# Low parts of the weights by a negation on ACT and an adding DMA, in place of a subtraction on DVE or POOL

## The chip, the cores and the metric

The kernel runs on one core of a Trainium2 chip. The metric is the device time of one execution in microseconds. Three runs of the kernel before gave 1173.53, 1174.44 and 1174.82 us; their median is 1174.44 us.

## What is computed

The reference is a two-layer trunk on 512 tokens of width 1024. Layer 0 is a gated short convolution beside a 4-head attention to 256 memory rows; then an MLP with a squared ReLU. After it, shared keys and values are made from the residual stream. Layer 1 (called layer B here) is differential attention over these keys beside memory attention, and again the MLP:

```python
for l in range(DEPTH):
    h = rmsnorm(x, norm_mix[l])
    proj = h @ (a_w_in[l] if l < N_A_LAYERS else b_w_q[j])
    ...
    main = short_conv_mixer(...) or diff_attention(q1, q2, k1, k2, v, lam)
    mo = memory_attention(qm, mem_n, w_mem_kv[l], ...)
    x = x + concatenate([main, mo]) @ w_o[l]
    x = x + square(relu(rmsnorm(x, norm_mlp[l]) @ w_up[l])) @ w_down[l]
    if l == N_A_LAYERS - 1:
        kv = rmsnorm(x, kv_norm) @ w_kv
```

Everything is float32, and the kernel keeps float32 accuracy by splitting each operand of a product into a high part (rounded to the type fp32r) and a low part (what the rounding left).

## The kernel before

All weights lie in DRAM in the order of their use, cut into **units**: eight 128x128 blocks that make one 128-row output tile. `UNITS` lists them: queries, convolution, memory keys and values, output projection, `up` and `dn` of the first MLP, then `qB`, `qk`, `kk`, `kv` for layer B, `wo1`, `wo2`, and the second MLP. A unit has two **halves** of four blocks (128x512 elements, 256 KB).

`dma_to` loads a unit into a tile `raw` (three buffers), one load of 512 KB from the queue of SP (L231) or two of 256 KB (L235). For the kinds `qB`, `kv`, `qk`, `kk`, POOL multiplies each loaded half in place by a gain (L241).

`prep_to` makes a half ready for TensorE: ACT copies `raw` into `wh`, rounded (L258), and then `wl = raw - wh` is one subtraction (L260). It runs on DVE, but on POOL for `wo1` and for the first `up` unit of the second MLP (`side`). `wh` and `wl` have four buffers each. Each half is prepared three halves ahead of its use (`AHEAD`), so the buffers that a preparation writes are those of the half that has just been used up. A unit's load is asked for one unit ahead of the preparation, and it waits until the last reader of the `raw` tile three units back is done.

`product` issues three matmuls for each block, into one PSUM bank: high by high (L276), the activations' low part by `wh` (L277), and the activations' high part by `wl` (L278). A half takes twelve matmuls of 512 columns.

Attention, norms and roots are generators with due times (`later`, `drive`), which put their instructions between the blocks of products. In layer B, POOL also does the rotary part of queries and keys (L926 to L928, behind a shuffle on DVE, L925) and clears tiles for the attention (L662, L663); in `wo1` it adds the residual (L955, L956). Each engine's queue takes its instructions in one order, which the framework sets when the kernel is built.

Of the kernel before, what the change touches and what calls it, by code (L numbers as in the profile page):

```python
# [10 lines left out]
F32 = mybir.dt.float32  # L11
F32R = mybir.dt.float32r
AF = mybir.ActivationFunctionType
ALU = mybir.AluOpType
# [20 lines left out]
WO_B = (2, 3)  # L35
SEG = 4
AHEAD = 3
LO_ON_POOL = ("wo1",)
WARM = 9

SUMS, ROOTS, NEXT_ROOT, VT = 5, 8, 3, 2
# [20 lines left out]
def _unit_list():  # L62

    u = []
    u += [("qmA", t, KT) for t in range(2)]
    for m in range(NH):
        if m == MEMA:
            u += [("mkv", 0, t, KT) for t in range(4)]
        if m == MEMB:
            u += [("mkv", 1, t, KT) for t in range(4)]  # L70
        u += [("win", CONV + m * P, KT), ("win", 2 * CONV + m * P, KT), ("win", m * P, KT)]
    u += [("woA", d, KT) for d in range(KT)]

    def mlp(l):
        r = []
        for q in range(NF):
            r += [("up", l, q * KT + f, KT) for f in range(KT)]
            r += [("dn", l, q, d, KT) for d in range(KT)]
        return r

    u += mlp(0)
    u += [("qB", 768 + t * P, KT) for t in range(2)]
    for p, t in LAYER_B:
        if t < 4:
            u += [("qk" if t < 2 else "kk", p * P + (t % 2) * 64, KT)]
        else:
            u += [("kv", 768 + (2 * p + t - 4) * P, KT)]
    u += [("wo1", i, KT) for i in range(len(WO1) // KT)]
    u += [("wo2", i, KT) for i in range(len(WO2) // KT)]
    u += mlp(1)  # L90
    return u


UNITS = _unit_list()
# [95 lines left out]
def trunk_kernel(ctx: ExitStack, tc: tile.TileContext, xT, memT, wall, cst, shp, csn, out):  # L190
    nc = tc.nc
    act, dve, pool, pe = nc.scalar, nc.vector, nc.gpsimd, nc.tensor
# [23 lines left out]
    side = next(i for i, u in enumerate(UNITS) if u[:2] == ("up", 1))  # L216
# [5 lines left out]
    def dma_to(n, between=()):  # L222
        between = list(between)
        while st["dma"] <= min(n, len(UNITS) - 1):
            i = st["dma"]
            kind, nb = UNITS[i][0], UNITS[i][-1]
            r = wpool.tile([P, KT, P], F32, tag="raw", name="raw", bufs=3)
            src = wall[OFFS[i] : OFFS[i] + P * P * nb].rearrange("(p b n) -> p b n", p=P, n=P)
            step = SEG if i < 2 or kind in ("qB", "kv", "qk", "kk") else nb
            if step == nb:  # L230
                nc.sync.dma_start(out=r[:, :nb, :], in_=src)  # L231
            for b0 in range(0, nb, step):
                rs = r[:, b0 : min(nb, b0 + step), :]
                if step < nb:
                    nc.sync.dma_start(out=rs, in_=src[:, b0 : min(nb, b0 + step), :])  # L235
                    for f in between[:2]:
                        f()
                    between = between[2:]
                if kind in ("qB", "kv", "qk", "kk"):
                    g0 = C_MIX1 if kind in ("qB", "qk") else C_KV  # L240
                    pool.tensor_tensor(  # L241
                        out=rs, in0=rs,
                        in1=cs[:, g0 + b0 : g0 + b0 + step].unsqueeze(2).to_broadcast([P, step, P]),
                        op=ALU.mult)
            st["raw"][i] = r
            st["dma"] += 1

    def prep_to(n):
        while st["prep"] <= min(n, len(halves) - 1):
            i, h = halves[st["prep"]]  # L250
            dma_to(i + 1)
            r = st["raw"][i]
            b0, b1 = h * SEG, min(UNITS[i][-1], h * SEG + SEG)
            rs = r[:, b0:b1, :]
            wh = wpool.tile([P, SEG, P], F32R, tag="wh", name="wh", bufs=4)
            wl = wpool.tile([P, SEG, P], F32R, tag="wl", name="wl", bufs=4)
            n_ = b1 - b0
            act.activation(out=wh[:, :n_, :], in_=rs, func=AF.Copy)  # L258
            eng = pool if i == side or UNITS[i][0] in LO_ON_POOL else dve
            eng.tensor_tensor(out=wl[:, :n_, :], in0=rs, in1=wh[:, :n_, :].bitcast(F32), op=ALU.subtract)  # L260
            st["w"][(i, h)] = (wh, wl)
            st["prep"] += 1

# [2 lines left out]
    def weights(b):  # L266

        i, b = cur["u"] + b // KT, b % KT
        prep_to(first[(i, b // SEG)] + AHEAD)
        wh, wl = st["w"][(i, b // SEG)]  # L270
        return wh[:, b % SEG, :], wl[:, b % SEG, :]
# [8 lines left out]
    def gemm_pieces(ps, srcs, order=range(KT), step=1, cols=slice(None)):  # L280

        u = cur["u"]
        cur["u"] += cols.stop in (None, S)
        for j, b in enumerate(order):
            prep_to(first[(u, b // SEG)] + AHEAD)
            wh, wl = (w_[:, b % SEG, :] for w_ in st["w"][(u, b // SEG)])
            product(ps, (wh, wl), [x_[:, cols] for x_ in srcs[b]], j == 0, j == len(order) - 1)
            if j % step == step - 1:
                yield
# [742 lines left out]
```

## Time and profile before

| | before |
|---|---|
| median of three runs | 1174.44 us |
| the profiled execution, its own time | 1173.49 us |
| its span, first to last instruction | 1171.7 us |
| busy: PE / DVE / ACT / POOL | 1140.6 / 697.4 / 526.3 / 191.2 us |
| the 16 DMA engines, share of the span in the queue of SP | 27.7% |
| subtractions on DVE and on POOL (L260) | 370 and 14 |

Busy times are sums of the instructions of an engine. PE is TensorE; its matmuls are pipelined, so that a row of some 390 ns stands for one that begins every 0.22 us or so. The word "released by" means that a semaphore of that instruction ended the wait. Times within the execution count from the start of the span.

### The profile page before, as it was taken

What the parts mean: (1) busy time and instruction counts of PE and PEld (TensorE: products, weight loads), DVE (VectorE), ACT (ScalarE), POOL (GpSimd) and SP (SyncE); (2) the same over time, 40 slices, a digit from 0 to 9 for tenths busy, and PEclk for the clock granted to TensorE, in tenths of its full rate; (3) what the DMA queues carried; (4) which work ended last, traced back from release to release, by engine and by line L of the source; (5) the groups of instructions that cost most, each with busy time, mean ns of one, the idle gap of its engine ahead of it and who ended that gap; (6) DMA issues with size and microseconds to landing.
All of it is one profiled execution on the core that took longest, in us unless ns stands there. A gap on an engine that the chain in (4) does not pass through costs nothing.

```text
span 1171.7 us, 14335 instructions
## 1 busy us (share of the span) xinstructions
PE 1140.6 (97%) x5343; PEld 931.3 (79%) x5343; DVE 697.4 (60%) x1124; ACT 526.3 (45%) x1013; POOL 191.2 (16%) x171
## 2 busy tenths in 40 slices
PE   8999999999999999999999889999999999999998
PEld 6888988888888888888777566767788888888887
DVE  7878664543443443446789999877743443443442
ACT  6655444432332432444556566676532432432431
POOL 3100002000000000005573744375200000000000
PEclk9999999999999999999999999999999999999999
DMA  8331323223223223232211111112232232322332
GB/s 270 107 121 60 118 99 100 98 90 105 93 92 106 90 97 101 90 107 91 91 54 37 55 55 42 50 55 72 90 108 91 95 103 91 106 92 92 106 109 72
DMA packets 35287, 108.38 MB, mean 93 GB/s; under 512 B 3985, under 2 KB 5521, under 8 KB 35217
## 3 DMA queue, kind: packets, MB, share of 16 engines
q1 hardware_dynamic: 35216, 107.47, 27.7%
q8 instruction: 42, 0.69, 0.2%
q14 instruction: 29, 0.23, 0.1%
HBM read 105.35 MB, written 2.10 MB: 92 GB/s over the span
## 4 chain that ended last, share of the span: by engine, by line
PE 82%; DVE 12%; ACT 2%; issue 1%; POOL 1%; DMA 0%; SPq 0%; DVEq 0%; POOLq 0%; ACTq 0%
PE g L276 26%; PE g L277 26%; PE g L278 26%; DVE wl L260 2%; DVE sl L490 1%; DVE pm L705 1%; DVE ql L344 1%; DVE dnb L697 1%; PE sc L576 1%; ACT pm L700 1%; DVE dsm L703 1%; DVE ra L413 1%; DVE xl L429 1%; PE msc L576 1%; DVE mp L619 1%
## 5 line engine op out<-in xcount | busy, mean ns | idle before, releaser
L258 ACT ACTIVATE wh<-raw 128x512 fp32r<-128x512 f32 x384 | 241.8, 630 | 484.0 <-PE g L277 427.2
L260 DVE TENSOR_TENSOR wl<-raw,wh 128x512 fp32r<-128x512 f32 x370 | 268.5, 727 | 175.6 <-ACT wh L258 175.2
L276 PE MATMUL g<-xh,wh 128*128 128x512 f32 x816 | 324.0, 397 | 0.4 <-DVE x L992 0.4
L277 PE MATMUL g<-xl,wh 128*128 128x512 f32 x816 | 321.0, 394 | 1.9 <-DVE xl L429 1.8
L278 PE MATMUL g<-xh,wl 128*128 128x512 f32 x816 | 319.6, 392 | 0.0
L276 PE MATMUL g<-hh,wh 128*128 128x512 f32 (+1 forms) x632 | 246.0, 389 | 1.8 <-ACT hh L343 1.8
L277 PE MATMUL g<-hl,wh 128*128 128x512 f32 (+1 forms) x632 | 244.9, 387 | 0.0
L278 PE MATMUL g<-hh,wl 128*128 128x512 f32 (+1 forms) x632 | 244.7, 387 | 0.0
L276 PEld LDWEIGHTS g<-xh,wh 128*128 128x128 f32 x816 | 154.3, 189 | 35.9 <-issue 2.7
L277 PEld LDWEIGHTS g<-xl,wh 128*128 128x128 f32 x816 | 154.3, 189 | 35.5 <-DVE xl L429 4.9
L278 PEld LDWEIGHTS g<-xh,wl 128*128 128x128 f32 x816 | 154.3, 189 | 32.3
L276 PEld LDWEIGHTS g<-hh,wh 128*128 128x128 f32 x632 | 119.1, 188 | 27.2 <-ACT hh L343 2.1
L278 PEld LDWEIGHTS g<-hh,wl 128*128 128x128 f32 x632 | 119.0, 188 | 24.0
L277 PEld LDWEIGHTS g<-hl,wh 128*128 128x128 f32 x632 | 119.1, 188 | 23.8 <-DVE hl L344 0.4
L762 DVE TENSOR_TENSOR x<-x,g 128x512 f32<-128x512 f32 (+1 forms) x65 | 44.2, 680 | 104.8 <-PE g L278 104.8
L752 DVE SCALAR_TENSOR_TENSOR v<-g,rstd 128x512 f32<-128x512 f32 x64 | 44.2, 691 | 90.6 <-PE g L278 90.6
L448 POOL TENSOR_TENSOR acc<-acc,sqf 128x512 f32<-128x512 f32 x18 | 25.2, 1398 | 368.3 <-ACT sqf L436 368.0
L755 DVE TENSOR_TENSOR hl<-a,hh 128x512 fp32r<-128x512 f32 x64 | 44.3, 693 | 37.8 <-ACT a L754 37.8
L241 POOL TENSOR_TENSOR raw<-raw,cs 128x512 f32<-128x512 f32 x40 | 46.7, 1186 | 34.1 <-DMA raw<-in_wall_dram 32.0
L753 ACT ACTIVATE hh<-v 128x512 fp32r<-128x512 f32 x64 | 40.4, 632 | 19.3 <-DVE v L752 19.3
L754 ACT ACTIVATE a<-v 128x512 f32<-128x512 f32 x64 | 39.4, 615 | 0.0
L700 ACT ACTIVATE pm<-sc,dnb 128x128 f32<-128x128 f32 (+3 forms) x48 | 25.0, 523 | 23.7 <-DVE dnb L697 23.6
(279 smaller groups left out, 1112.1 us busy)
## 6 DMA issues: line engine op xcount, KB each, us to landing
raw<-in_wall_dram SPq DMA_DIRECT2D x170, 512.0 KB, 3.5
raw<-in_wall_dram SPq DMA_DIRECT2D x44, 256.0 KB, 2.9
x<-in_xT_dram SPq DMA_DIRECT2D x8, 256.0 KB, 5.3
out_dram<-x SPq DMA_DIRECT2D x7, 256.0 KB, 2.0
mraw<-in_memT_dram SPq DMA_DIRECT2D x4, 256.0 KB, 5.8
rope<-in_csn_dram SPq DMA_DIRECT2D x2, 512.0 KB, 5.3
ind<-in_shp_dram SPq DMA_DIRECT2D x1, 256.0 KB, 5.6
out_dram<-x SPq DMA_DIRECT2D x2, 128.0 KB, 1.7
```

What stands on the lines that cost most here:

```text
L241: pool.tensor_tensor(out=rs, in0=rs, in1=cs[:, g0 + b0 : g0 + b0 + step].unsqueeze(2).to_broadcast([P, step, P]), op=ALU.mult)
L258: act.activation(out=wh[:, :n_, :], in_=rs, func=AF.Copy)
L260: eng.tensor_tensor(out=wl[:, :n_, :], in0=rs, in1=wh[:, :n_, :].bitcast(F32), op=ALU.subtract)
L276: pe.matmul(out=ps, lhsT=wh, rhs=xh, start=start, stop=False)
L277: pe.matmul(out=ps, lhsT=wh, rhs=xl, start=False, stop=False)
L278: pe.matmul(out=ps, lhsT=wl, rhs=xh, start=False, stop=stop)
L700: act.activation(out=pm[:, m, 0:n], in_=sc[m][:, 0:n], func=AF.Exp, bias=nb[:, m : m + 1], accum_out=sm[:, m : m + 1])
L752: dve.scalar_tensor_tensor(out=v, in0=ps, scalar=0.0, in1=rstd, op0=ALU.max, op1=ALU.mult)
L753: act.activation(out=hh, in_=v, func=AF.Square)
L754: act.activation(out=a, in_=v, func=AF.Square)
L755: dve.tensor_tensor(out=hl, in0=a, in1=hh.bitcast(F32), op=ALU.subtract)
L762: dve.tensor_tensor(out=x[d][:, c], in0=x[d][:, c], in1=ps[:, c], op=ALU.add)
```

## The change

For every half, ACT first writes `-raw`, rounded to fp32r, into `wl`; then a DMA issued from the queue of POOL adds `raw` to `wl` in place, which leaves the same rest; then ACT makes `wh` as before. No subtraction is left on DVE or POOL, and `LO_ON_POOL` goes.

```diff
-LO_ON_POOL = ("wo1",)
...
             n_ = b1 - b0
+            act.activation(out=wl[:, :n_, :], in_=rs, func=AF.Copy, scale=-1.0)
+            pool.dma_start(out=wl[:, :n_, :].bitcast(F32), in_=rs, accum_op=ALU.add)
             act.activation(out=wh[:, :n_, :], in_=rs, func=AF.Copy)
-            eng = pool if i == side or UNITS[i][0] in LO_ON_POOL else dve
-            eng.tensor_tensor(out=wl[:, :n_, :], in0=rs, in1=wh[:, :n_, :].bitcast(F32), op=ALU.subtract)
```

The line numbers move by one or two: in the changed kernel the negation is L259, the adding DMA L260, the rounding copy L261, the gain on POOL L240. The queues change as follows. In the rows, numbers tell one tile from another, and a name in brackets is a semaphore: `DMAHW` of a DMA of SP, `DMASW` of an adding DMA, the others of an engine.

POOL at the start of the program, before (the squares of the first five tiles of `x`, then the gate of a convolution):

```order
L663 MEMSET tl_5555 128x128
L438 ISA
L438 TENSOR_TENSOR acc_193<-x_105 128x512 [waits DMAHW2_49]
L438 TENSOR_TENSOR sqf_195<-x_106 128x512 [waits DMAHW3_49]
L438 TENSOR_TENSOR sqf_198<-x_107 128x512 [waits DMAHW5_49]
L438 TENSOR_TENSOR sqf_201<-x_108 128x512 [waits DMAHW6_49]
L438 TENSOR_TENSOR sqf_204<-x_109 128x512 [waits DMAHW0_49]
L829 TENSOR_TENSOR qp_441<-qp_441,qp_393 128x512 [waits DVE_49]
```

POOL at the same place, now:

```order
L664 MEMSET tl_5779 128x128
L260 DMA wl_251<-raw_132 128x512 [waits DMAHW1_49,Activation_49]
L439 ISA
L439 TENSOR_TENSOR acc_193<-x_105 128x512 [waits DMAHW2_49]
L439 TENSOR_TENSOR sqf_195<-x_106 128x512 [waits DMAHW3_49]
L439 TENSOR_TENSOR sqf_198<-x_107 128x512 [waits DMAHW5_49]
L439 TENSOR_TENSOR sqf_201<-x_108 128x512 [waits DMAHW6_49]
L439 TENSOR_TENSOR sqf_204<-x_109 128x512 [waits DMAHW0_49]
L260 DMA wl_256<-raw_132 128x512 [waits DMAHW4_49,Activation_49]
L260 DMA wl_261<-raw_139 128x512 [waits DMAHW7_49,Activation_49]
L260 DMA wl_266<-raw_139 128x512 [waits DMAHW2_49,Activation_49]
```

The first adding DMA stands ahead of the squares, the next three behind all five of them.

POOL where the gains of the first units of layer B are multiplied in (units `qB` and `qk`), before:

```order
L241 TENSOR_TENSOR raw_4709<-raw_4709,cs_95 128x512 [waits DMAHW6_49,DVE_49]
L241 TENSOR_TENSOR raw_4709<-raw_4709,cs_95 128x512 [waits DMAHW7_49]
L241 TENSOR_TENSOR raw_4765<-raw_4765,cs_95 128x512 [waits DMAHW0_49,DVE_49]
L241 TENSOR_TENSOR raw_4765<-raw_4765,cs_95 128x512 [waits DMAHW1_49]
L241 TENSOR_TENSOR raw_4814<-raw_4814,cs_95 128x512 [waits DMAHW2_49,DVE_49,Pool_49]
L241 TENSOR_TENSOR raw_4814<-raw_4814,cs_95 128x512 [waits DMAHW3_49]
```

POOL at the same place, now (the units' tiles are, in order, raw_4762, raw_4808, raw_4854, raw_4913, raw_4971):

```order
L260 DMA wl_4838<-raw_4762 128x512 [waits Activation_49]
L240 TENSOR_TENSOR raw_4854<-raw_4854,cs_95 128x512 [waits DMAHW4_49,DMASW7_49,DMASW6_49]
L449 TENSOR_TENSOR acc_4570<-acc_4570,sqf_4833 128x512 [waits Activation_49]
L240 TENSOR_TENSOR raw_4854<-raw_4854,cs_95 128x512 [waits DMAHW5_49]
L260 DMA wl_4860<-raw_4808 128x512 [waits Activation_49]
L240 TENSOR_TENSOR raw_4913<-raw_4913,cs_95 128x512 [waits DMAHW6_49,DMASW1_49,DMASW0_49]
L260 DMA wl_4897<-raw_4808 128x512 [waits Activation_49,Pool_49]
L240 TENSOR_TENSOR raw_4913<-raw_4913,cs_95 128x512 [waits DMAHW7_49]
L260 DMA wl_4919<-raw_4854 128x512 [waits Activation_49,Pool_49]
L240 TENSOR_TENSOR raw_4971<-raw_4971,cs_95 128x512 [waits DMAHW0_49,DMASW3_49,DMASW2_49]
L260 DMA wl_4949<-raw_4854 128x512 [waits Activation_49,Pool_49]
```

The multiplication of raw_4913, which is loaded into the buffer that raw_4762 leaves, stands ahead of the second adding DMA of raw_4808; that of raw_4971 ahead of the second one of raw_4854; and so on down the layer.

TensorE at the start, now:

```order
L277 MATMUL g_249<-xh0_161,wh_250 128x512 [waits Activation_49]
L278 MATMUL g_249<-xl0_169,wh_250 128x512 [waits DVE_49]
L279 MATMUL g_249<-xh0_161,wl_251 128x512 [waits DMASW0_49]
L277 MATMUL g_249<-xh1_162,wh_250 128x512 [waits Activation_49]
L278 MATMUL g_249<-xl1_170,wh_250 128x512 [waits DVE_49]
```

The third matmul of each half's first block waits for an adding DMA, where it waited for DVE or POOL.

## The prediction

> **What bounds the kernel now.** I read the busy times stage by stage first; columns are stretch and length, then busy time and instructions of PE, PEld, DVE, ACT and POOL, the granted clock, the DMA engines' share and GB/s.
>
> ```profile
> 0.00:30.00 30.00, 26.71 (x91) 20.02 (x92) 21.94 (x31) 18.50 (x33) 8.79 (x19) 1.00 0.82 272
> 30.00:540.00 510.00, 509.59 (x2405) 424.77 (x2404) 274.54 (x428) 213.61 (x383) 23.44 (x17) 1.00 0.30 98
> 540.00:575.00 35.00, 35.00 (x155) 28.71 (x154) 24.14 (x32) 18.26 (x31) 17.60 (x16) 1.00 0.29 91
> 575.00:705.00 130.00, 115.50 (x600) 89.80 (x599) 121.57 (x211) 76.76 (x185) 77.12 (x65) 0.97 0.16 53
> 705.00:840.00 135.00, 125.26 (x627) 95.03 (x626) 115.86 (x216) 91.19 (x209) 64.23 (x56) 0.99 0.18 60
> 840.00:1145.00 305.00, 305.00 (x1348) 252.62 (x1347) 132.50 (x199) 104.83 (x172) 0.00 (x0) 1.00 0.30 101
> ```
>
> From 30 to 575 and from 840 on TensorE never pauses, and DVE, ACT and POOL have room: nothing is won there. Layer B (575 to 840) is another matter: PE idles 14.5 and 9.7 us, and DVE is busy for 121.57 of 130 us. The chain that ended last, cut to 575 to 705, names the subtraction first:
>
> ```profile
> by line: DVE wl L260 12.4%; DVE sl L490 7.2%; issue 7.0%; DVE ql L344 6.1%; DVE pm L705 5.1%; DVE mp L619 4.5%; DVE rp L925 4.1%; DVE dnb L697 3.7%; DVE hl L344 3.3%; DVE dsm L703 3.2%; DVE qp L516 2.9%; DVE qp L921 2.9%; ACT pm L700 2.6%;
> ```
>
> That is 16 us of chain that the change may take away. Then who releases the loads, from the waits of SP's queue (total, times, longest):
>
> ```profile
> SPq L231 <- DVE wl L260: 786.2, 158, 11.6
> SPq L235 <- DVE wl L260: 140.2, 19, 12.4
> ```
>
> So `wl` does more than feed TensorE: when it is done, the `raw` tile is free and the load of three units later starts.
>
> **The change, part by part.** The groups that are removed or copied, and the window rows of L260 (stretch, length, DVE, POOL):
>
> ```profile
> L258 ACT ACTIVATE wh<-raw 128x512 fp32r<-128x512 f32 x384 | 241.8, 630 | 484.0 <-PE g L277 427.2
> L260 DVE TENSOR_TENSOR wl<-raw,wh 128x512 fp32r<-128x512 f32 x370 | 268.5, 727 | 175.6 <-ACT wh L258 175.2
> L241 POOL TENSOR_TENSOR raw<-raw,cs 128x512 f32<-128x512 f32 x40 | 46.7, 1186 | 34.1 <-DMA raw<-in_wall_dram 32.0
> ...
> 575.00:705.00 130.00, 22.89 (x25) 0.00 (x0) 0.97 0.16 53
> 705.00:840.00 135.00, 16.72 (x18) 18.91 (x14) 0.99 0.18 60
> 840.00:1145.00 305.00, 77.83 (x113) 0.00 (x0) 1.00 0.30 101
> ```
>
> DVE loses 268.5 us, of which only 22.89 + 16.72 us lie where DVE limits. ACT gains 384 x 0.630 = 242 us: in 575 to 705 that is 25 x 0.63 = 16 on 76.76 of 130 us, in 705 to 840 32 x 0.63 = 20 on 91.19 of 135, in 840 to 1145 113 x 0.63 = 71 on 104.83 of 305. None fills, so I cost ACT at nothing; what hides it is the idle in those rows, and if it were late, the exponentials of layer B (pm L700) would be late next. POOL gains 384 issues and loses 14 subtractions; in 575 to 705 that is 25 issues on 77.12 of 130 us, room again, but a queue with waits in it (below). `wh` comes 0.63 us later, against a lead of three halves.
>
> The unknown is the adding DMA. Call **p** the time from the end of the negation to the sum's landing, with its issue on POOL. No row shows such a DMA. The nearest (size, median us from issue to landing):
>
> ```profile
> raw<-in_wall_dram SPq DMA_DIRECT2D x170, 512.0 KB, 3.5
> raw<-in_wall_dram SPq DMA_DIRECT2D x44, 256.0 KB, 2.9
> x<-in_xT_dram SPq DMA_DIRECT2D x8, 256.0 KB, 5.3
> out_dram<-x SPq DMA_DIRECT2D x7, 256.0 KB, 2.0
> mraw<-in_memT_dram SPq DMA_DIRECT2D x4, 256.0 KB, 5.8
> ```
>
> Lower end 2.0 (a 256 KB transfer that reads SBUF); upper end 5.8 for a crowded one plus 1.0 of POOL (its multiplication of such a tile takes 1.04 us in rows below), 6.8. I take 2.9 + 1.0 = **3.9**, since the load of the same size into the same memory is nearest, and POOL's share of an issue is unknown but hardly less than 0 or more than a pass over the tile.
>
> The Trainium skill, "DMA: Bandwidth & Descriptors", section on the anatomy of a DMA on the GpSimd path, fits plain copies with 2.0 us plus bytes over 436 GB/s: for 256 KB that is an estimate of 2.6 us. No run here shows it yet, and SP's 256 KB loads take 2.9. By 2.6 the sum below would be about -9 us, by 3.9 it is +20.
>
> *The MLPs.* Preparations come one half apart:
>
> ```profile
> 539.23 0.63 ACT L258 ACTIVATE wh<-raw 128x512 fp32r<-128x512 f32 x1 [2.09 <-PE g L277]
> 541.95 0.63 ACT L258 ACTIVATE wh<-raw 128x512 fp32r<-128x512 f32 x1 [0.61 <-PE g L277]
> 544.67 0.63 ACT L258 ACTIVATE wh<-raw 128x512 fp32r<-128x512 f32 x1 [2.09 <-PE g L277]
> ```
>
> A half lasts 2.72 us, the lead is 8.16. Negation 0.63 plus p = 3.9 leaves 3.6 us; up to p = 7.5 TensorE sees nothing. The load, released 3.9 instead of 0.7 us after ACT, lands 3.5 later, at 8.0 of the 13.6 us (five halves) until its own preparation. Cost 0. ACT also rounds the hidden tiles, but keeps 305 - 176 = 129 us of idle in 840 to 1145.
>
> *The start.* The negation ends where `wh` did, and the sum lands 3.9 us later:
>
> ```profile
> 4.12 0.63 ACT L258 ACTIVATE wh<-raw 128x512 fp32r<-128x512 f32 x1 [0.98 <-DMA raw<-in_wall_dram]
> 7.57 0.63 PE L278 MATMUL g<-xh,wl 128*128 128x512 f32 x1
> 11.31 0.80 PE L277 MATMUL g<-xl,wh 128*128 128x512 f32 x1 [1.25 <-DVE xl L429]
> 14.04 0.83 PE L278 MATMUL g<-xh,wl 128*128 128x512 f32 x2
> 8.10 4.06 POOL L438 TENSOR_TENSOR sqf<-x 128x512 f32<-128x512 f32 x3 [0.28 <-DMA x<-in_xT_dram]
> ```
>
> The first sum is there at 8.65, not 7.57: 1.1 us, which the wait for `xl` at 11.31 partly swallows. The second is issued behind the squares, at 12.16, and lands at 16.1 instead of the 14.04 at which its kind was used; TensorE has other blocks for about a microsecond. I take **+2** (0 to +5, as the DMA engines are 82% busy here).
>
> *540 to 575, the first units with a gain.* Here the order of POOL's queue matters. The multiplication of unit j+3 stands ahead of the second adding DMA of unit j+1, it needs the load of j+3, and that load needs the second `wl` of unit j. So the sums now hang on one another around a ring: sum of j, load, multiplication, sum of j+1. Before, `wl` was on DVE and the ring was open. The rows of one link:
>
> ```profile
> 540.06 0.74 DVE L260 TENSOR_TENSOR wl<-raw,wh 128x512 fp32r<-128x512 f32 x1
> 540.83 1.77 SPq L235 DMA_DIRECT2D raw<-in_wall_dram  x2
> 538.22 2.04 POOL L241 TENSOR_TENSOR raw<-raw,cs 128x512 f32<-128x512 f32 x2 [0.95 <-DMA raw<-in_wall_dram]
> 544.02 1.04 POOL L241 TENSOR_TENSOR raw<-raw,cs 128x512 f32<-128x512 f32 x1 [1.32 <-DMA raw<-in_wall_dram]
> 545.37 1.04 POOL L241 TENSOR_TENSOR raw<-raw,cs 128x512 f32<-128x512 f32 x1 [0.31 <-DMA raw<-in_wall_dram]
> 572.26 2.04 POOL L241 TENSOR_TENSOR raw<-raw,cs 128x512 f32<-128x512 f32 x2 [4.46 <-DMA raw<-in_wall_dram]
> 703.61 1.04 POOL L241 TENSOR_TENSOR raw<-raw,cs 128x512 f32<-128x512 f32 x1
> ```
>
> `wl` ends at 540.80, the first half is multiplied from 544.02: 3.2 us; plus 1.04; plus p: one turn takes 4.3 + p = 8.2 us. TensorE wants a unit each (572.26 - 538.22) / 6 = 5.67 us. Six turns fall 6 x 2.5 = 15 us behind, less the slack of 3.6: **+11** (at p = 2.0, 3.6 behind with 5.5 of slack, 0; at 6.8, 32.6 - 0.7 = +32).
>
> *575 to 705.* Thirteen units, 131.4 us to the last multiplication above, 10.1 each. Here both multiplications stand ahead of the second sum in most turns: second half multiplied from 545.37, 4.6 us after the release, plus 1.04, plus p = 9.5 us. POOL's other work in this stretch:
>
> ```profile
> L926 POOL TENSOR_TENSOR rp<-rp,rope 128x512 f32<-128x512 f32 x10 | 16.7, 1667 | 31.1 <-DVE rp L925 29.2 <-PE sc L576 1.9
> ```
>
> It waits 29 us for DVE's shuffles, and the adding DMAs queued behind that wait too; the load's flight covers most of it, and I add 1.0 us a turn (half of 29 over 13 units). 10.5 x 13 = 136.5: **+5**. Without the ring the stage would shrink, DVE's 121.57 falling to 98.7, to PE's 115.5: that is the lower end, -14.5; at p = 6.8 it is 13.4 x 13 - 131 = +43.
>
> *705 to 840.* POOL's 14 subtractions (1.35 us each) become issues, the sums land some 2.6 us later than those, behind residual additions that wait for ACT; DVE gets 16.72 us free, and PE idles 9.7. I take **+2** (-3 to +8).
>
> Sum: 2 + 11 + 5 + 2 = +20. The profiled execution took 1173.49 us by its own clock, 1.8 more than its span and 0.95 less than the median; added to the median 1174.44 it gives **1195**. Lower bound 0 + 0 - 14.5 - 3 = -17, 1157; upper 5 + 32 + 43 + 8 = +88, 1262.
>
> **Rivals.**
>
> 1. *The short DMA: faster.* The terms change sign together: at p = 3.0 they are about 1 + 5 - 6 + 0 = 0, so this decides between the signs. At p = 2.0 the ring turns in 6.3 us, inside the slack, and layer B shrinks to PE's floor: 1157. At 2.6: 1 + 2 - 11 - 1 = -9, 1165. For it speaks the 2.0 of `out_dram<-x`; against it that every row that writes SBUF shows 2.9 or more. The page named above would have this rival right. Chance 0.25.
>
> 2. *The ring is covered.* Relief in DVE pays for what POOL costs, within 0.2%, which is about what this measurement can tell from no change. That needs p within 0.1 of 3.0, or an attention that has slack I don't see: 0.05.
>
> 3. *ACT takes DVE's place in layer B.* If all 25 + 32 negations there lay on the path, 36 us: about 1210. Against it: the chain above holds ACT at 2.6% for its largest line. Chance 0.10, slower.
>
> 4. *The DMA engines fill.* The loads take 0.30 of them in the MLPs. The adding DMAs move as many bytes again; at the loads' price that makes 0.60, and they fill only if a byte costs 2.4 times as much. At three times the share is 1.2, and the 815 us of 30 to 540 and 840 to 1145 stretch by a fifth, +163, 1337. Chance 0.08. The Trainium skill's same page ("Issuing engines are not separate DMA queues") says that DMAs of all issuers run on the same 16 engines; it gives no price for an adding one, and no row here has one.
>
> My forecast, slower by the ring of POOL's queue, holds 0.52. That the change doesn't do what it says is excluded by the queues: each `wl` matmul now waits for a DMA.
>
> **How the numbers follow.** Faster 0.25 (rival 1), same 0.05 (rival 2), slower 0.52 + 0.10 + 0.08 = 0.70. The range leaves out rival 4 and the last of rival 1: 1162 to 1262. The forecast's own range is 1180 (p = 3.3) to 1262.
>
> **What would show it.** Right: the adding DMA's median landing near 3 to 5 us; loads in SP's queue released by a DMA; PE idle in 540 to 575, waiting at its `wl` matmul; POOL's multiplications 8 us apart there; the MLP rows as before; DVE well under 100 of 130 us from 575 on. Wrong: landings under 2 us and layer B shorter (rival 1), ACT full there (3), or PE pausing in the MLPs with the DMA share near 1 (4).

## The result, and the profile after

The changed kernel takes 1210.82 us (median of four runs, 1210.24 to 1211.44); the kernel before takes 1173.99 us in the same comparison. The ratio is 1.0316, with a 95% interval of 1.0299 to 1.0334: 37 us slower. The forecast was 1195, slower, with a range of 1162 to 1262.

The page of the changed kernel: busy times, then the two DMA queues with packets, MB and the share of 16 engines' span:

```profile
PE 1149.1 (95%) x5343; PEld 933.1 (77%) x5343; DVE 458.4 (38%) x754; ACT 713.7 (59%) x1397; POOL 486.2 (40%) x541
...
q0 software_dynamic: 55296, 100.69, 48.7%
q1 hardware_dynamic: 35216, 107.47, 27.8%
```

From its list of DMA issues, the size and the median us from issue to landing:

```profile
wl<-raw POOLq DMA_DIRECT2D x384, 256.0 KB, 3.9
```

DVE lost 239 us of busy time and ACT gained 187. That is less than the rows of the subtractions (268.5) and of the negations (236.8) add up to, in part because the rows of neighbouring instructions overlap. The adding DMA's median landing is the 3.9 us that the prediction took for p, over the whole run: it is 6.5 us from 0 to 36 and 3.3 us from 610 to 740. But it occupies the DMA engines more than a load does: 48.7% for 100.69 MB against 27.8% for 107.47 MB, so a byte costs 1.87 times as much.

The largest entry among the waits of SP's queue shows who releases the loads now (total, times, longest):

```profile
SPq L230 <- DMA wl<-raw: 907.9, 169, 12.0
```

Then the stretches of the changed kernel, with columns as in the prediction's first fence; the stages lie later, so the bounds of 565, 610, 740, 875 and 1180 answer to its 540, 575, 705, 840 and 1145, and its one row from 30 to 540 is split here:

```profile
0.00:30.00 30.00, 22.05 (x72) 16.06 (x73) 16.56 (x20) 19.20 (x37) 12.51 (x25) 1.00 0.97 293
60.00:90.00 30.00, 25.98 (x153) 22.81 (x152) 11.14 (x18) 19.26 (x36) 11.13 (x14) 0.94 0.94 210
150.00:180.00 30.00, 25.31 (x145) 21.47 (x144) 8.43 (x13) 18.32 (x33) 11.55 (x13) 1.00 0.96 203
...
240.00:565.00 325.00, 325.00 (x1436) 269.10 (x1435) 68.69 (x100) 175.12 (x312) 106.38 (x122) 1.00 0.87 194
565.00:610.00 45.00, 38.68 (x157) 29.77 (x156) 16.48 (x21) 24.73 (x45) 25.96 (x27) 0.96 0.60 136
610.00:740.00 130.00, 116.01 (x595) 89.58 (x595) 108.04 (x185) 86.62 (x206) 90.47 (x91) 0.95 0.48 107
740.00:875.00 135.00, 122.44 (x623) 94.69 (x624) 95.19 (x195) 105.78 (x240) 71.70 (x76) 0.96 0.55 123
875.00:1180.00 305.00, 305.00 (x1347) 252.41 (x1346) 61.27 (x89) 161.35 (x287) 96.52 (x113) 1.00 0.86 193
```

The MLPs run without a pause at a DMA share of 0.86 to 0.87. But between 60 and 90, and between 150 and 180, PE now idles 4 to 5 us of 30. The kernel before, in the same two stretches, had no such pause, at shares of 0.37 and 0.30:

```profile
60.00:90.00 30.00, 30.00 (x181) 25.61 (x179) 23.86 (x37) 17.52 (x35) 1.61 (x1) 1.00 0.37 123
150.00:180.00 30.00, 30.00 (x133) 24.60 (x132) 17.04 (x27) 11.30 (x19) 3.00 (x2) 1.00 0.30 101
```

Landmarks tell where the lag grows. Each is the start (us) of one DVE or ACT instruction found by its line in both traces:

| | before | after | lag | growth |
|---|---|---|---|---|
| first query unit done | 30.3 | 36.8 | 6.5 | +6.5 |
| last convolution unit done | 152.7 | 171.3 | 18.6 | +12.1 |
| first hidden tile of MLP 0 | 217.1 | 242.6 | 25.5 | +6.9 |
| last hidden tile of MLP 0 | 512.3 | 537.5 | 25.2 | -0.3 |
| last residual addition of MLP 0 | 555.8 | 583.7 | 27.9 | +2.7 |
| first `qk` unit done | 573.7 | 608.4 | 34.7 | +6.8 |
| first `kv` unit done | 609.9 | 646.8 | 36.9 | +2.2 |
| last residual addition of `wo1` | 805.3 | 839.3 | 34.0 | -2.9 |
| first hidden tile of MLP 1 | 835.1 | 871.5 | 36.4 | +2.4 |
| last residual addition | 1168.6 | 1206.0 | 37.4 | +1.0 |

Two thirds of the loss lie in layer A, which the prediction costed at 2 us. Most of the rest arises where the first MLP goes over into the units with a gain; what follows takes and gives back 3 us at the most.

### The profile page after: what moved, and what is told of

Same layout as the page of the kernel before. It is cut to its first block, busy times and chain, and to the rows that moved or that the text cites. A ratio compares the mean times of both kernels' runs of the same rounds, so it can differ in the third digit from the quotient of the medians.

```text
span 1209.5 us, 15529 instructions
## 1 busy us (share of the span) xinstructions
PE 1149.1 (95%) x5343; PEld 933.1 (77%) x5343; DVE 458.4 (38%) x754; ACT 713.7 (59%) x1397; POOL 486.2 (40%) x541
## 3 DMA queue, kind: packets, MB, share of 16 engines
q0 software_dynamic: 55296, 100.69, 48.7%
q1 hardware_dynamic: 35216, 107.47, 27.8%
## 4 chain that ended last, share of the span: by engine, by line
PE 58%; issue 12%; DVE 8%; DMA 8%; ACT 7%; POOL 7%; POOLq 0%; SPq 0%; ACTq 0%; DVEq 0%
PE g L279 18%; PE g L277 18%; PE g L278 18%; DMA wl<-raw 6%; POOL wl L260 5%; DMA raw<-in_wall_dram 2%; ACT wl L259 1%; ACT pm L701 1%; DVE sl L491 1%; DVE pm L706 1%; DVE dnb L698 1%; POOL acc L449 1%; ACT wh L261 1%; DVE mp L620 1%; DVE ql L345 1%
## 5 line engine op out<-in xcount | busy, mean ns | idle before, releaser
L260 POOL DMA_DIRECT2D wl<-raw x384 | 334.9, 878 | 633.1 <-ACT wl L259 578.0
L261 ACT ACTIVATE wh<-raw 128x512 fp32r<-128x512 f32 x384 | 241.6, 629 | 369.2 <-PE g L278 261.8
L259 ACT ACTIVATE wl<-raw 128x512 fp32r<-128x512 f32 x384 | 236.8, 617 | 15.0 <-DMA raw<-in_wall_dram 6.3
L240 POOL TENSOR_TENSOR raw<-raw,cs 128x512 f32<-128x512 f32 x40 | 48.0, 1229 | 48.6 <-DMA raw<-in_wall_dram 48.6
```

Source lines behind the costliest of these rows:

```text
L240: pool.tensor_tensor(out=rs, in0=rs, in1=cs[:, g0 + b0 : g0 + b0 + step].unsqueeze(2).to_broadcast([P, step, P]), op=ALU.mult)
L259: act.activation(out=wl[:, :n_, :], in_=rs, func=AF.Copy, scale=-1.0)
L260: pool.dma_start(out=wl[:, :n_, :].bitcast(F32), in_=rs, accum_op=ALU.add)
```

## The experiments

Unless said otherwise, an experiment keeps the changed kernel for some kinds of units and returns to the subtraction for the others. The condition stands in `prep_to`; "old" is ACT's copy and the subtraction on DVE (on POOL where the kernel before had it), "new" the negation, the adding DMA and the copy. Differences in us below are differences of the ratios to the kernel before, times 1174 us. A ratio's interval reaches 0.001 to 0.0034 to each side, mostly some 2 us, and landmarks come from one execution each; 2 or 3 us between two kernels mean little.

### Layer A: memory units, all units, first units, output projection

```diff
+if UNITS[i][0] == "mkv": old          # e1
+if UNITS[i][0] in ("qmA", "win", "mkv", "woA"): old   # e2
+if UNITS[i][0] == "qmA": old          # e10
+if UNITS[i][0] == "woA": old          # e11
```

The memory's keys and values alone:

> The changed kernel, but the memory keys' and values' units (8 of 192) subtract on DVE again. Theory (short halves): these units have 256 columns, so a half lasts some 1.4 us instead of 2.72 and the three halves of lead are 4.1 us, less than the negation plus the adding DMA, while the DMA engines are at 0.94; all of the 11.6 us that the changed kernel loses between its first and its last convolution unit arises here: about 1199 us, PE without pauses at 60 to 90. Rival (the DMA's latency costs everywhere in layer A, or ACT's doubled work does): the 16 halves are a tenth of layer A's, so 1 to 4 us come back: 1207 to 1210.

Measured 1201.71 us, ratio 1.0241 [1.0222, 1.026], between the two but nearer to the theory. PE no longer pauses from 60 to 90.

All of layer A:

> The changed kernel, but all units of layer A up to its output projection subtract on DVE again (qmA, win, mkv, woA). If the first 240 us alone hold the loss of 25 us seen there between the two traces, about 1186 us; what stays, some 12 us, is the ring in the units with a gain and what follows it. Rival (the loss merely moves, since a later stage waits for the same thing anyway): nearer to 1200.

Measured 1187.08 us, 1.0127 [1.0099, 1.0154].

The first two units:

> The changed kernel, but the first two units (the queries, four halves) subtract on DVE. Theory (the start loses its 6.5 us to the first sums, which land late among the loads of the activations, and that delay is carried to the end): 1203.5 to 1206, first query unit at some 31 us. Rival (the delay at the start is swallowed by the stall of the memory units that follows): 1208.5 to 1211.

Measured 1206.33 us, 1.0277 [1.0257, 1.0297].

The output projection:

> The changed kernel, but the eight units of layer A's output projection subtract on DVE. Theory (they lose 5 to 7 us because their blocks are used out of order, which shortens the lead): 1203.5 to 1206. Rival (those microseconds are arrears of the memory units' loads and come with any kind of preparation): 1208.5 to 1211. With the start (6.5) and the memory units (9.1) the three are to add up to some 21 to 24, which is what all of layer A gave.

Measured 1206.45 us, 1.0285 [1.026, 1.0309].

Layer A as a whole is worth 22 us (1.0316 - 1.0127), the memory units 9, the start 4.6, the output projection 3.6. The last two fell a little short of what was expected, by less than their intervals, and their sum with the memory units is 17, not 21 to 24. At the first hidden tile of MLP 0 the traces do add up: the three edits stand there 12.4, 5.8 and 6.6 us ahead of the changed kernel, together 24.8 of its lag of 25.5. So little is left for the `win` units, and some of what an edit gains in layer A is lost again behind it; what takes it back was not tried apart.

What the start lost is visible in two rows of the changed kernel, the issue of the first adding DMA on POOL and the matmul that waits for it:

```profile
5.17 1.00 POOL L260 DMA_DIRECT2D wl<-raw  x1 [2.50 <-ACT wl L259]
13.44 0.79 PE L279 MATMUL g<-xh,wl 128*128 128x512 f32 x1 [1.71 <-DMA wl<-raw]
```

8.3 us from issue to use, at a DMA share of 0.97; the kernel before used this `wl` at 7.57. TensorE's wait of 1.71 us is only the end of it, because the matmul ahead was late as well:

```profile
10.93 0.80 PE L278 MATMUL g<-xl,wh 128*128 128x512 f32 x1 [4.09 <-DVE xl L430]
6.02 4.85 DVE L430 SCALAR_TENSOR_TENSOR xl<-x,cs,xh 128x512 fp32r<-128x512 f32 x1 [3.42 <-ACT xh L429]
```

DVE's first `xl` took 1.35 us before and takes 4.85 now, beside POOL's squares, which follow the first adding DMA without a gap (last section). The sum lands later still, so it sets the 13.44.

### Full DMA engines or too short a lead?

In a memory unit the products are 256 columns wide, and the halves follow one another faster. ACT's preparations in the kernel before:

```profile
61.89 0.63 ACT L258 ACTIVATE wh<-raw 128x512 fp32r<-128x512 f32 x1 [0.66 <-ACT wh L258]
63.34 0.63 ACT L258 ACTIVATE wh<-raw 128x512 fp32r<-128x512 f32 x1 [0.82 <-PE g L277]
```

A half takes 1.45 us, so three halves of lead are 4.4 us. Two explanations were open: the engines are full there, or a sum is too long for such a lead however idle they are.

```diff
-pool.dma_start(out=wl[:, :n_, :].bitcast(F32), in_=rs, accum_op=ALU.add)
+m_ = 1 if UNITS[i][0] == "mkv" else n_
+pool.dma_start(out=wl[:, :m_, :].bitcast(F32), in_=r[:, b0 : b0 + m_, :], accum_op=ALU.add)
```

> The changed kernel, but in the memory's key and value units each sum covers one block of four (the low parts of the other three blocks keep only the negation, so that part of the product is left out). Number and order of the sums stay, their bytes there fall to a quarter. Theory of full DMA engines in 53 to 171 us: the DMA share there falls from .95 to about .7, the landings to about 3.5 us, and the time to 1200 to 1204. Rival (the fixed part of a sum, its issue and its shortest landing of some 3.3 us, is already too long for the 4.1 us that the three halves ahead give): 1207 to 1211.

Measured 1205.28 us, 1.0269 [1.0251, 1.0288], between the two. The landings from 60 to 90, first of the changed kernel, then of this one:

```profile
wl<-raw POOLq DMA_DIRECT2D x13, 256.0 KB, 4.9
```

```profile
wl<-raw POOLq DMA_DIRECT2D x7, 256.0 KB, 4.7
wl<-raw POOLq DMA_DIRECT2D x7, 64.0 KB, 3.5
```

With a quarter of the bytes 5.5 us come back, where 8.8 came back when the memory units had no adding DMA at all. So some half of that loss or more is bytes on crowded engines; the intervals of 2 us allow no closer share. The rest goes with the sums themselves: 64 KB still take 3.5 us to land here. Both explanations have a part.

### The gain and the units that need it

```diff
-                    pool.tensor_tensor(
+                    dve.tensor_tensor(          # e3: the gain, L240
...
+if UNITS[i][0] in ("qB", "kv", "qk", "kk"): old          # e4
```

> The changed kernel, but DVE instead of POOL multiplies the gain into the loaded halves of qB, kv, qk, kk. Ring theory (POOL's queue holds an adding DMA back behind a multiplication that waits for a load that waits for an earlier adding DMA): the ring opens, the units with a gain follow TensorE again at about 5.5 us each up to layer B's first attention, and about 9 us come back; POOL's runs also get shorter, so DVE's stretched instructions (up to 5.5 us) become fewer: 1195 to 1202 in all. Rival (the adding DMA's landing alone is late, whatever POOL does): the link load, multiplication, sum stays, 1207 to 1212; DVE's 40 more instructions (some 30 us) may even make it 1215.

Measured 1199.11 us, 1.0218 [1.0198, 1.0238].

> The changed kernel, but the units with a gain (qB, kv, qk, kk) subtract on DVE again; layer A, both MLPs, wo1 and wo2 keep the adding DMA. Ring theory: the 9.5 us between the first multiplication and the first attention come back, and from 605 to 750 the stage is as long as before, since there the two traces are level: about 1201. Rival (DVE's relief had been paying there): the stage gets longer by up to the 22.9 us that DVE's subtractions took, and the total is at 1205 to 1215.

Measured 1199.98 us, 1.0221 [1.0187, 1.0255].

Either edit opens the ring that the prediction described, and both give back 11 us. Not all of it is the ring's. From the last hidden tile of MLP 0 to the first `kv` unit the lag grows by 11.7 us in the changed kernel, by 4.9 in e3 and by 6.6 in e4; so 5 to 7 us come back there and the rest only behind it, where both edits also make instructions of DVE shorter (last section). POOL's queue in the changed kernel shows it, gain and adding DMA in turn:

```profile
568.93 1.03 POOL L240 TENSOR_TENSOR raw<-raw,cs 128x512 f32<-128x512 f32 x1 [4.88 <-DMA raw<-in_wall_dram]
569.92 0.86 POOL L260 DMA_DIRECT2D wl<-raw  x1
...
576.78 1.03 POOL L240 TENSOR_TENSOR raw<-raw,cs 128x512 f32<-128x512 f32 x1 [2.85 <-DMA raw<-in_wall_dram]
577.77 0.86 POOL L260 DMA_DIRECT2D wl<-raw  x1
...
614.91 2.48 POOL L240 TENSOR_TENSOR raw<-raw,cs 128x512 f32<-128x512 f32 x2 [4.17 <-DMA raw<-in_wall_dram]
```

The gain waits for a load, and the sum behind it in the queue is issued as the gain ends. Six units later the gain stands at 614.91: 7.7 us a unit, against 5.67 before.

### The MLPs alone

```diff
+if UNITS[i][0] not in ("up", "dn") or i == side: old
```

> Adding DMAs in both MLPs alone (the unit at the side and all other units as before). The term of the prediction (the MLPs lose nothing, the lead of 8.16 us covers 0.63 + 3.9): 1172 to 1176, with at most 3 us at the end of the first MLP, where the gains of the next units stand in POOL's queue among the last sums. Rival (the MLPs' sums cost the 7 us by which the changed kernel with layer A undone, 1187.1, stands above the one with adding DMAs in layer B alone, 1180.2, whatever layer B does): 1179 to 1182.

Measured 1181.49 us, 1.0057 [1.0035, 1.0079]. The number of the rival came out, but its place is not within the MLPs. A stretch of this kernel inside the MLP and the one at its end:

```profile
300.00:500.00 200.00, 200.00 (x884) 165.78 (x883) 40.08 (x58) 107.09 (x190) 62.78 (x73) 1.00 0.87 196
540.00:575.00 35.00, 30.94 (x121) 24.41 (x120) 20.93 (x21) 14.80 (x26) 21.32 (x18) 0.90 0.44 119
```

The seam at 540 to 575 loses it. Its rows on POOL, where L240 is the gain, L265 the adding DMA and L454 the sum of squares for the next norm, and then PE's:

```profile
543.30 1.03 POOL L240 TENSOR_TENSOR raw<-raw,cs 128x512 f32<-128x512 f32 x1 [4.01 <-DMA raw<-in_wall_dram]
544.29 0.86 POOL L265 DMA_DIRECT2D wl<-raw  x1
544.90 1.33 POOL L240 TENSOR_TENSOR raw<-raw,cs 128x512 f32<-128x512 f32 x1
545.90 1.57 POOL L454 TENSOR_TENSOR acc<-acc,sqf 128x512 f32<-128x512 f32 x1
547.14 1.18 POOL L265 DMA_DIRECT2D wl<-raw  x1
```

```profile
552.78 0.51 PE L284 MATMUL g<-hh,wl 128*128 128x512 f32 x1 [1.58 <-DMA wl<-raw]
566.53 0.79 PE L467 MATMUL ss<-al,onesr 128*128 128x512 f32 x1 [1.73 <-DVE al L350]
```

The last sums of the MLP stand behind a gain that waits 4 us for its load. The one issued at 547.14 is still awaited at 552.78. The norm's squares stand in the same queue, and PE then waits for the norm, at 566. By the landmarks the lag at the first `qk` unit is 8.2 us (581.9 against 573.7). No adding DMA of a unit with a gain is needed for this: one queue that holds both gains and sums is enough.

### Layer B alone, and where the adding DMA might pay

```diff
+if UNITS[i][0] not in ("qB", "kv", "qk", "kk", "wo1", "wo2") and i != side: old   # e5, e9
-                    pool.tensor_tensor(
+                    dve.tensor_tensor(          # e9 as well: the gain
+if UNITS[i][0] not in ("wo1", "wo2"): old   # e6
```

> Adding DMAs only in layer B's units (qB, kv, qk, kk, wo1, wo2) and in the first half pair of the last MLP; every other unit subtracts as before. Theory (the MLPs lose nothing, layer A loses some 25 us, the ring of POOL's queue 9 to 10, the unit at the side 3): 1173 + 12 = 1184 to 1188, first MLP v to last qB some 350 plus 5 to 6 as with layer A alone undone. Rival (the MLPs' own sums cost something that the later stages' slack hides, so that layer A, the ring and the MLPs don't add up): below 1181.

Measured 1180.22 us, 1.0053 [1.0032, 1.0074]. The theory missed and the rival's figure came out: with the MLPs' sums gone too, 8.7 us more come back than with layer A undone alone, and the last query unit is done at 567.1, as in the kernel before. The loss comes later: the first `kv` unit is 6.0 us behind. The ring does turn in this kernel. Its seventh unit's gain begins at

```profile
583.88 2.48 POOL L240 TENSOR_TENSOR raw<-raw,cs 128x512 f32<-128x512 f32 x2 [4.06 <-DMA raw<-in_wall_dram]
```

46.0 us after the first unit's at 537.89: 7.7 us a unit again, and 11.6 us later than the 572.26 of the kernel before. So the gains fall behind as the prediction worked out, but at the first `kv` unit TensorE is only half as late.

> As the kernel with adding DMAs in layer B alone, and the gain multiplication of the scaled units on DVE in place of POOL, so that POOL's queue holds only the sums there. Theory (the ring through POOL's queue is load, gain, sum in one queue; without the gain it is gone): 1173 to 1178. Rival (the landing of the sum itself, not the queue, paces these units): 1183 to 1188, as without this edit.

Measured 1171.92 us, 0.9985 [0.9974, 0.9995]. That is a little below the theory's range: taking the gain out of POOL's queue gives back 8 us here as well. By the first `kv` unit it is 2.4 us, the rest comes later.

> Adding DMAs only in wo1 and wo2; all others subtract as before, the unit at the side on POOL. Theory (there DVE is freed while nothing but these units' own sums is in POOL's queue; with the scaled units undone the stretch from the first qk to the last x add of wo1 took 224.6 us against 231.6 before): 1166 to 1170, faster than before. Rival (that 224.6 came from the scaled units' other place of work or from the later start of the stretch, and wo gains nothing): 1172 to 1176.

Measured 1166.76 us, 0.9944 [0.9929, 0.996]: 0.6% faster than the kernel before. But the adding DMA was not shown to be the reason, since it also takes twelve subtractions off POOL. The last experiment is the kernel before without any adding DMA:

```diff
-LO_ON_POOL = ("wo1",)
+LO_ON_POOL = ()
```

> The kernel before, with the subtractions of wo1 on DVE in place of POOL (LO_ON_POOL empty). No adding DMA. It tells why the kernel with adding DMAs in wo1 and wo2 alone gained 6.6 us. Theory (work is taken off DVE and POOL together): 1173 to 1180, no gain. Rival (it was enough to take the twelve subtractions off POOL, whose queue then does the rotary part and the residual additions sooner): 1166 to 1170.

Measured 1166.61 us, 0.9949 [0.9931, 0.9967]. The theory fell and the rival held: DVE does these subtractions, and the whole gain is there. Two stretches, of the kernel before, of e6 and of e12:

```profile
755.00:785.00 30.00, 28.16 (x140) 20.52 (x140) 22.12 (x54) 21.40 (x59) 20.72 (x20) 0.94 0.16 54
785.00:815.00 30.00, 27.68 (x154) 22.70 (x151) 23.63 (x35) 19.08 (x41) 15.64 (x11) 1.00 0.17 53
```

```profile
755.00:785.00 30.00, 29.12 (x151) 21.39 (x152) 23.39 (x56) 25.54 (x63) 18.97 (x21) 1.00 0.49 107
785.00:815.00 30.00, 29.50 (x160) 24.78 (x159) 19.89 (x32) 24.35 (x50) 20.64 (x17) 1.00 0.47 114
```

```profile
755.00:785.00 30.00, 29.95 (x151) 22.04 (x150) 25.19 (x62) 23.39 (x60) 13.67 (x14) 1.00 0.15 54
785.00:815.00 30.00, 29.21 (x163) 24.33 (x162) 24.15 (x40) 21.32 (x45) 14.55 (x11) 1.00 0.22 71
```

DVE (third pair of numbers) had room here all along: it takes the twelve over and rises by 3 us in the first stretch and half a microsecond in the second, and PE pauses less.

## Why the prediction was right or wrong

**The sign was right, and so was p in the median.** The median landing is 3.9 us, and no sum landed in under 3.2. The time lies within the range partly by luck: of the 37 us, 22 come from layer A, and the range reached so far up for a longer p in layer B.

The Trainium skill ("DMA: Bandwidth & Descriptors", the anatomy of a DMA on the GpSimd path) gives by its fit an estimate of 2.6 us for such a size. The section does not speak of adding DMAs, and this trace does not bear the figure out for them; rival 1, which needs such a landing, falls.

**The ring at 540 to 575, +11: it turns as worked out, but the size came out partly by luck.** The gains were 7.7 us apart where 8.2 were worked out, and the lag grows by 11.7 us from the last hidden tile of MLP 0 to the first `kv` unit. But the prediction put all of that down to the sums of the units with a gain. These alone, in e5, lose nothing at the first `qk` unit and 6 us by the first `kv` unit, so the slack was larger than the 3.6 us of the sum. The MLPs' last sums in the same queue, which it did not count, are enough to lose 8 us at the seam.

**"The MLPs: cost 0" holds inside them.** From the first to the last hidden tile of MLP 0 the changed kernel takes 294.9 us, the kernel before 295.2. At the seam the MLPs' sums do cost something, as just told.

**The failed step is layer A.** The prediction read "from 30 to 575 TensorE never pauses" and "DVE, ACT and POOL have room", and then took the MLPs' 8.16 us of lead and the mean DMA share of 0.30 for the whole stretch. Neither holds in layer A. The lead is half as long in the memory units, and there the kernel before already loaded at up to twice the mean share:

```profile
60.00:70.00 10.00, 10.00 (x82) 9.82 (x81) 6.99 (x12) 7.02 (x12) 0.00 (x0) 1.00 0.60 200
140.00:150.00 10.00, 10.00 (x71) 9.22 (x69) 7.17 (x11) 7.23 (x13) 0.00 (x0) 1.00 0.50 162
```

p is longer there too: the landings' median is 4.9 us from 60 to 90 and 5.5 from 150 to 180. The start was taken at +2; the trace shows +6.5, and undoing it gave 4.6. Everything from the first query unit to the first MLP was not costed at all, and it is +19 in the trace. Why the output projection loses, where the products are 512 columns wide, is not shown; that its blocks are used out of order, as expected before e11, is only argued. An average over 510 us hid the two short stretches of high demand.

**575 to 705, +5, and 705 to 840, +2: too high.** From the first `kv` unit to the last residual addition of `wo1` the lag falls by 2.9 us, and from the first `qk` unit, with which the stretch begins, by 0.7. The prediction looked for DVE well under 100 of 130 us here, and it shows 108.04. Two effects of opposite sign were missed. DVE's instructions became longer (last section), so that its relief was small. And taking the twelve subtractions off POOL is worth 6 us by itself; the prediction saw them become issues and gave no credit for it.

**Rivals.** Rival 3 named the right time, 1210, for a wrong reason: ACT was busy 86.62 of 130 and 105.78 of 135 us there, and e9, which keeps all negations of layer B, takes 1171.92 us, no longer than the kernel before. Rival 4 set its threshold at 2.4 times a load's byte; it is 1.87, and 0.30 x 2.87 gives the 0.86 measured in the MLPs, so the engines do not fill there. Its mechanism is real where the demand is higher: at a share of 0.94 it has a part in the memory units' loss, as the quarter sums show.

**The balance**, by ratios: layer A 22, the MLPs' sums 7 and layer B's 6 (with its 6 to 7 of gain in `wo` already in it) make 35 of the 37 us, each to some 2 us.

## What to carry to other kernels

A mean over a long stretch with no pauses does not show where the spare time is thin; go through it in windows of the size of one stage, with the lead and the DMA share of each, before an added latency is costed at nothing. When work moves into a queue, look for whatever in that queue waits for a transfer which in turn waits for the moved work, and for what belongs to the next stage (here the norm's squares) and stands behind it. And when an edit replaces two things, undo them apart: the only gain that these runs show came from taking twelve subtractions off POOL, which one line does without any DMA.

## What was not expected of the hardware

DVE's instructions with two inputs in SBUF became longer while POOL ran gains and rotary products one behind the other. One group in layer B, four instructions of equal shape (busy time, mean ns): first the kernel before, then the changed kernel, then the changed kernel with the gain on DVE:

```profile
L619 DVE TENSOR_TENSOR mp<-mp,sm 128x1024 f32<-128x1024 f32 x4 | 6.0, 1510 | 0.1
```

```profile
L620 DVE TENSOR_TENSOR mp<-mp,sm 128x1024 f32<-128x1024 f32 x4 | 9.3, 2322 | 0.1
```

```profile
L620 DVE TENSOR_TENSOR mp<-mp,sm 128x1024 f32<-128x1024 f32 x4 | 4.9, 1217 | 0.0
```

The longest single case in the changed kernel, and POOL's rows beside it:

```profile
743.62 5.50 DVE L641 SCALAR_TENSOR_TENSOR ob<-ob,sub_g,ra 128x512 f32<-128x512 f32 x1
```

```profile
742.89 2.32 POOL L240 TENSOR_TENSOR raw<-raw,cs 128x512 f32<-128x512 f32 x2
744.88 1.17 POOL L260 DMA_DIRECT2D wl<-raw  x1
745.49 1.86 POOL L927 TENSOR_TENSOR rp<-rp,rope 128x512 f32<-128x512 f32 x1
746.71 1.85 POOL L928 TENSOR_TENSOR qp<-qp,rope 128x512 f32<-128x512 f32 x1
748.63 1.60 POOL L929 TENSOR_TENSOR qp<-qp,rp 128x512 f32<-128x512 f32 x1
```

The mean of that DVE line over layer B was 0.93 us before. The instruction ends half a microsecond after POOL's third rotary product has begun, so it seems to have been held up across several of POOL's instructions, not one. The gains alone do not do it: with the sums of these units back on DVE (e4) the group takes 1.52 us, as in the kernel before. It takes 2.25 us or more in every run that has both these gains and these sums in POOL's queue, and 1.52 or less in every other. The Trainium skill ("SBUF — State Buffer", who interferes with whom) says that a DVE instruction with two SBUF inputs contends with a GpSimd instruction that reads SBUF, since they share a read interface. The trace agrees: the group above falls from 2.32 to 1.22 us when the gains leave POOL. Whether this has a part in `wo`'s gain from an idler POOL is not shown: in e12 the group stays at 1.51 us, and the DVE line of the single case falls from 0.93 to 0.74.
